# Five edits to a tuned decoder-layer kernel: one joint triangular substitution, w_o's rows behind the merge, a later T4, a moved subtraction, and a norm weight spread by products

## The chip, the cores and the metric

One core of a Trainium2 chip runs the whole kernel. The metric is device time in microseconds from start to end of one execution, as a median over runs.

The engines are named as in the profile's rows: PE is TensorE (matrix products), DVE is VectorE, ACT is ScalarE, POOL is GpSimd, and SP is the engine whose queue issues most of the transfers. Each engine works through its own instructions in their order, and waits at an instruction whose inputs or whose target buffer are not ready.

## The reference, cut to what matters

One decoder layer on 1024 tokens of width 1024, float32 in and out:

```python
u = rmsnorm(h, norm_mix_pre)
parts = split(u @ w_in)                  # q, k, v, z, b, a for mixer A; the rest for mixer B and the gates
ya = gdn_mixer(...)                      # causal conv over 4 tokens, silu, l2norm, gated delta rule
yb = nsa_mixer(...)                      # compressed, selected and sliding-window attention
mixed = (sigmoid(ga) * (ya @ w_a2d) + sigmoid(gb) * (yb @ w_b2d)) @ w_o
h = h + rmsnorm(mixed, norm_mix_post)
f = causal_dwconv(rmsnorm(h, norm_ffn_pre) @ w_up, conv_ffn) + conv_ffn_b
f = (gelu(f_gate) * f_val) @ w_down      # 2816 wide
h = h + rmsnorm(f, norm_ffn_post)
h = h + rmsnorm((p @ w_ple) * sigmoid(h @ w_ple_gate), norm_ple_post)
```

Inside the delta rule each chunk of a head needs the inverse of a unit lower triangular matrix, `lower + I`, with `lower = beta * (k k^T) * decay`.

## The kernel before, in words

A library schedules the instructions. The Python code is written in one order, and the library fixes the order on each engine by its own estimate of times; `tc.issue_after(x)` and `self.behind(x, ...)` keep what is written under them behind the instruction x. Pools of buffers (`bufs=n`) add waits where a buffer has to come free.

Every product is made three times (`mm3`, L394 to L396): each operand is split into a high part, rounded by ACT (`hi`, `whi`, `whl`), and a low part, the difference, made by DVE or POOL (`lo_of`, L362). The products high by high, low by high and high by low are added in PSUM. The low parts are where DVE and POOL come in for nearly every weight.

The stages that the change touches:

- **Start.** `mixers` loads x, and a copy of the first norm's weight for each of 128 partitions (`wbc`, 512 KB, by one transfer from ACT's queue). `norm_to_T` scales each token tile by it (`xs_u`, L414), and PE turns it (`pT_u`, L423).
- **Convolution and inverse.** For each of 12 feature tiles `conv` multiplies u by a 128-column slice of w_in (`pj`, 48 matmuls), evacuates the product with ACT (`y`, L570), adds three shifted taps on DVE (L573) and applies silu. Tiles 4 to 7 are k, 0 to 3 q, 8 to 11 v. `norms` sums the squares (`pss`). `gdn_small` makes the decay and gate numbers. `gdn_inverse32` makes, for each of 8 chunks of 128 tokens, the product k k^T (`pkk`), the decay factors (`E`, L948 on DVE, then exp on ACT, L953) and `L`, two DVE operations (L984, L985); it stores L in DRAM and reads its 32x32 diagonal blocks back, so that a block lies in 4 partitions and 32 blocks fill 128. Then it solves all blocks by forward substitution: 31 steps of one product (L1003) and one subtraction (L1005). It does this in two halves, chunks 0 to 3 in 64 partitions and chunks 4 to 7 in the other 64, with 62 DVE operations each, and its `yield`s let the convolution's work come between. The result goes to DRAM (`xd`) and is read back as blocks (`blk`). Four z gate tiles (`yz`, L611) are multiplied, then `gdn_prep(0)` combines the blocks with products (`pz`, `pt`, `pt1n`, L961 and L1041), and the scan over chunks begins.
- **Merge.** 16 tiles of 128 features by 512 tokens: a gate (ACT sigmoid, L795), gate times mixer A's product (DVE, L815), the product with w_b2d (`pab` on PE, 12 matmuls a tile), gate times it (L818), their sum (L819), and its high part `mxh` (ACT, L821) and low part `mxl` (POOL, for the last four tiles DVE). w_b2d comes in four slices (`stream`, L369, L373), the last two of them loaded inside this loop. `open_wo` loads the first NWO = 4 of w_o's 8 rows of tiles ahead of the loop, and `ffn` the other four behind it; `product` multiplies a token tile by rows 0 to 3 (half 0), for three token tiles, and then by rows 4 to 7.
- **Up-projection.** A Strassen-like scheme over pairs of feature tiles: seven products of half size, with weight sums `s1` to `s4` (`sums`) and token sums T2, T3, T4 (`turn`, L253 to L257). In `rest` pairs 0 to 2 are written out by hand, the others in a loop. `copy_of` (L106) copies a product out of PSUM on ACT before more is added to it; `c22` (L179) adds such a copy `r` to the product `n` on DVE before `p4` adds to n. `block_sum` (L234) makes sums of activations on POOL between products.
- **Down product.** `down` runs seven products of 11 steps each. A step loads an activation tile, splits it (`whl`, low part on DVE) and splits a weight tile (`wdhl`, low part on POOL, L362), and does 12 matmuls. Between the steps DVE makes weight differences in place: in product 4 (`dq`, written over `Q`) both `b12 -= ...` and `b21 -= t2` (L1567, L1568).

## Time and profile before

| What | Value |
|---|---|
| Median of 3 runs | 1929.55 us (1926.06 to 1931.4) |
| The profiled execution's own time | 1925.03 us |
| Its span, first to last instruction | 1923.3 us |
| Mean granted clock of TensorE | 0.986 of full speed |
| Busy: PE, DVE, ACT, POOL | 95%, 65%, 48%, 36% |
| Instructions | 25903 |

[...] A matmul of 128x512 shows as 0.39 us busy, but the next one starts 0.23 us later, since they overlap. A row of the timeline has the start, the busy time, the engine, the line, what is written and read, the shape, and in square brackets the idle time ahead and what ended it. The waits add these up: for a tile of PE, which operation on which engine it waited for. The table of stretches gives the busy time of each engine in a window.

### The profile page before, as it was taken

Reading aid. Unit: us, or ns where it says so; the run is one execution under the profiler, and the core shown is the slowest. Engines: PE = TensorE matmul, PEld = TensorE weight load, DVE = VectorE, ACT = ScalarE, POOL = GpSimd, SP = SyncE. Lnnn points to the kernel's source line nnn. Section 1 sums busy time; section 2 is a strip of 40 time slices with the busy share of each in tenths; the row PEclk is TensorE's granted clock in tenths of the full one; section 3 lists DMA queues with packets and bytes.
Section 4 is the critical chain, followed back from the end, with each engine's and each line's share of the span. In section 5 each row is a group of like instructions: output and inputs, shape, how many; then the busy total and the mean of one; then the engine's idle time right before and its main releaser. Section 6 shows DMA issues by size and latency. Waiting matters only on the chain. (4 is left out here: it accounts for less than half of the span.)

```text
span 1923.3 us, 25903 instructions
## 1 busy us (share of the span) xinstructions
PE 1834.8 (95%) x9307; PEld 1524.8 (79%) x9307; DVE 1242.5 (65%) x2353; ACT 919.2 (48%) x1817; POOL 700.2 (36%) x527
## 2 busy tenths in 40 slices
PE   7999989999999999999889998999999999899998
PEld 7888778988888888778768886787878877677786
DVE  5437934441367667766786589888777775948643
ACT  4344223323367667766664245444444444446432
POOL 2132112224122112331153146666666664645200
PEclk9999999999999999999999999999999999999999
DMA  5124333333310100110065212223332256246201
GB/s 168 34 86 116 91 92 89 93 88 92 102 45 18 45 29 34 57 44 13 22 216 169 98 55 94 98 94 101 107 99 93 99 206 243 77 138 219 76 34 44
DMA packets 182622, 178.67 MB, mean 93 GB/s; under 512 B 27549, under 2 KB 133342, under 8 KB 182494
## 3 DMA queue, kind: packets, MB, share of 16 engines
q1 hardware_dynamic: 180272, 170.33, 28.3%
q10 hardware_dynamic: 2222, 6.69, 0.9%
q8 instruction: 73, 1.20, 0.2%
q14 instruction: 55, 0.45, 0.1%
HBM read 132.65 MB, written 44.34 MB: 92 GB/s over the span
## 5 line engine op out<-in xcount | busy, mean ns | idle before, releaser
L394 PE MATMUL pj<-uh,whi 128*128 128x512 f32 x640 | 259.1, 405 | 7.4 <-DVE y L573 4.5
L395 PE MATMUL pj<-ul,whi 128*128 128x512 f32 x640 | 255.5, 399 | 0.0
L396 PE MATMUL pj<-uh,wlo 128*128 128x512 f32 x640 | 254.9, 398 | 0.0
L362 POOL TENSOR_TENSOR wlo<-raw,whi 128x1024 fp32r<-128x1024 f32 x48 | 117.5, 2449 | 312.1 <-ACT whi L373 268.3
L394 PEld LDWEIGHTS pj<-uh,whi 128*128 128x128 f32 x640 | 121.4, 190 | 35.4 <-issue 4.5
L362 POOL TENSOR_TENSOR whl<-s,whl 128x512 fp32r<-128x512 f32 x84 | 119.5, 1425 | 70.8 <-ACT whl L1393 69.0
L396 PEld LDWEIGHTS pj<-uh,wlo 128*128 128x128 f32 x640 | 121.2, 189 | 28.5
L395 PEld LDWEIGHTS pj<-ul,whi 128*128 128x128 f32 x640 | 121.4, 190 | 25.7
L362 POOL TENSOR_TENSOR whl<-raw,whl 128x512 fp32r<-128x512 f32 x71 | 114.6, 1621 | 62.6 <-ACT whl L1393 62.0
L362 POOL TENSOR_TENSOR wdhl<-wd,wdhl 128x512 fp32r<-128x512 f32 x66 | 100.0, 1524 | 82.2 <-ACT wdhl L1393 78.9
L362 DVE TENSOR_TENSOR whl<-araw,whl 128x512 fp32r<-128x512 f32 x77 | 89.8, 1173 | 54.9 <-ACT whl L1393 54.8
L394 PE MATMUL q<-mxh,whl 128*128 128x512 f32 (+1 forms) x272 | 105.9, 394 | 7.7 <-ACT r L106 7.7
L1275 ACT ACTIVATE Pt<-Pt,nm 128x640 f32<-128x640 f32 (+7 forms) x128 | 93.0, 729 | 36.4 <-DVE nm L1273 35.9
L1305 DVE TENSOR_TENSOR Tl<-pt,Th 128x512 fp32r<-128x512 f32 (+1 forms) x152 | 92.5, 616 | 21.7 <-ACT Th L1304 17.3
L396 PE MATMUL q<-mxh,whl 128*128 128x512 f32 (+1 forms) x272 | 105.1, 387 | 0.7 <-POOL whl L362 0.7
L395 PE MATMUL q<-mxl,whl 128*128 128x512 f32 (+1 forms) x272 | 105.3, 387 | 0.0
L1304 ACT ACTIVATE Th<-pt 128x512 fp32r<-128x512 f32 (+1 forms) x152 | 78.5, 539 | 42.7 <-PE po L1308 33.4
L373 ACT ACTIVATE whi<-raw 128x1024 fp32r<-128x1024 f32 x48 | 50.5, 1053 | 85.5 <-PE pj L395 55.5
L1301 PE MATMUL pt<-ident,Pt 128*128 128x128 f32 x528 | 83.4, 277 | 5.1 <-DVE Tl L1305 3.2
L1343 POOL TENSOR_TENSOR tm<-tm 128x128 f32<-128x128 f32 x32 | 14.8, 462 | 195.1 <-DVE tm L1341 155.3
L152 DVE SCALAR_TENSOR_TENSOR yg<-c,cv,yg 128x511 f32<-128x511 f32 (+2 forms) x88 | 76.9, 875 | 2.1 <-ACT yg L149 1.8
L152 DVE SCALAR_TENSOR_TENSOR yv<-c,cv,yv 128x1023 f32<-128x1023 f32 (+1 forms) x44 | 65.7, 1492 | 15.7 <-ACT yv L149 13.4
(548 smaller groups left out, 5181.4 us busy)
## 6 DMA issues: line engine op xcount, KB each, us to landing
raw<-in_w_up SPq DMA_DIRECT2D x44, 512.0 KB
raw<-in_w_in SPq DMA_DIRECT2D x40, 512.0 KB
araw<-acts SPq DMA_DIRECT2D x35, 512.0 KB
acts<-sd SPq DMA_DIRECT2D x44, 256.0 KB
gates_d<-yz SPq DMA_DIRECT2D x40, 256.0 KB
acts<-yv SPq DMA_DIRECT2D x33, 256.0 KB
gt<-gates_d SPq DMA_DIRECT2D x32, 256.0 KB
wd<-in_w_down SPq DMA_DIRECT2D x7, 1024.0 KB
```

The costliest lines, as they stand in the source:

```text
L152: self.body.nc.vector.scalar_tensor_tensor(y, src, w, y, ALU.mult, ALU.add)
L362: return eng.tensor_sub(lo, src, hi.bitcast(F32)).ins
L373: nc.scalar.activation(hi, raw, AF.Copy)
L394: nc.tensor.matmul(ps, lh, rh, start=start, stop=False, skip_group_check=more)
L395: nc.tensor.matmul(ps, lh, rl, start=False, stop=False, skip_group_check=more)
L396: nc.tensor.matmul(ps, ll, rh, start=False, stop=stop, skip_group_check=more)
L1275: nc.scalar.activation(Pt[:, hh, 0:nk], Pt[:, hh, 0:nk], AF.Exp, scale=2.0 ** -(h0 + hh + 1), bias=nm[:, br, hh:hh + 1], accum_out=rs[:, b ...
L1301: nc.tensor.transpose(pt[:, b, hh], Pt[:, hh, (b0 + b) * P:(b0 + b + 1) * P], self.ident)
L1304: nc.scalar.activation(Th[:, 0:m], pt[:, 0:m], AF.Copy)
L1305: nc.vector.tensor_sub(Tl[:, 0:m], pt[:, 0:m], Th[:, 0:m].bitcast(F32))
L1343: nc.gpsimd.tensor_add(tm[:, 0], tm[:, 0], tm[:, 1])
```

## The change

1. **Start.** The weight is loaded once, as 1x1024; two float32 products of a row of ones (1x128) with its halves spread it over the partitions in PSUM, and two DVE copies bring it to SBUF.
2. **Inverse.** `a_log` and `dt_bias` are loaded in the first stage. `gdn_small` becomes a generator that runs in three parts behind tiles 1 and 2. `E` of the noncausal kind is one ACT operation per head (Relu with the bias -gc). L is one DVE operation per head. All 8 chunks come first, two for each convolution tile, then one substitution over 128 partitions with three yields. `gdn_prep(0)` starts behind the second of the four z gate tiles.
3. **Merge.** NWO is 2; the last two slices of w_b2d are asked for earlier, and all these low parts are DVE's. Rows 2 to 7 of w_o load behind the merge, and `product` takes rows 0 to 3 one at a time over three token tiles.
4. **Up-projection.** Pair 1's s4 and the T4 turns are tied behind the copy r too, and pair 2 takes no block sum between its products.
5. **Down product.** `b21 -= t2` moves from product 4 to product 3.

The diff, cut to its core:

```diff
-NWO = 4
+NWO = 2
...
-        with body.behind(t3):
+        with body.behind(t3, self.copied):
             self.sums(b, (4,))
             t4 = self.turn(t2s, 4, range(4))
...
-                if self.todo:
+                if self.todo and n > 2:
...
-                    nc.scalar.dma_start(wbc, rows_to_all(io["norm_mix_pre"], DM))
+                    row, one = [self.wp.tile([P, DM], F32, name=n, tag=t, bufs=2)[0:1] for n, t in
+                                (("wrow", "raw"), ("one", "hi"))]
+                    nc.scalar.dma_start(row, rows_to_all(io["norm_mix_pre"], DM)[0:1])
+                    nc.vector.memset(one[:, 0:P], 1.0)
+                    for hf in range(2):
+                        c, ps = slice(hf * 512, hf * 512 + 512), self.psg.tile([P, 512], F32, name="pwb", tag="g")
+                        nc.tensor.matmul(ps, one[:, 0:P], row[:, c], start=True, stop=True)
+                        nc.vector.tensor_copy(wbc[:, c], ps)
                 self.norm_to_T(x, wbc, uh, ul, t, xw, self.psg, f"u{t}")
...
+            if inv:
+                with self.behind(last["DVE"], self.mm_last, *self.inv_last):
+                    next(inv, None)
             if n and order[n - 1] < 8:
                 norms(order[n - 1])
+            run_all(cv)
+            if n == 1:
+                self.gp = self.g1 = self.pool(ges, "gdn")
+                small = self.gdn_small(pss)
+            if n in (1, 2):
+                with self.behind(*last.values(), self.mm_last):
+                    next(small)
             if order[n - 1] == 7:
-                inv = self.gdn_inverse32()
-            if inv:
-                next(inv, None)
-            run_all(cv)
-        run_all(inv)
+                run_all(small)
+                inv, self.inv_last = self.gdn_inverse32(), ()
+        with tc.issue_after(last["DVE"]):
+            run_all(inv)
         jes.close()
         fes = ExitStack()
         psF = [self.pool(fes, "psF", 2, space=PSUM, side="right")]
...
             run_all(gate_tile(n))
+            if n == 1:
+                with tc.issue_after(self.mm_last):
+                    self.gdn_prep(0)
         NG = 8
-        self.gdn_prep(0)
...
+                if th and f % 2 and f0 + 4 < KD:
+                    wbs.append(self.stream(wbd, 0, 4, (f0 + 4) * P, 2 * P, nc.vector))
...
-            if f0 + 4 < KD:
-                wbs.append(self.stream(wbd, 0, 4, (f0 + 4) * P, 2 * P))
...
+            j = slice(c * H + h, c * H + h + 1)
+            if causal:
+                nc.vector.tensor_scalar(E[:, h], gr[:, h], self.gc[:, j], 0.0, ALU.subtract, ALU.min)
+            else:
+                nc.scalar.activation(E[:, h], gr[:, h], AF.Relu, bias=self.ngc[:, j])
...
+        for c in range(NC):
+            rk = self.row4(1, c, "qk", 2)
+            gr = self.row4(0, c, "gr", 2)
+            k = self.chunk(1, c)
+            nc.vector.tensor_mul(k, k, rk)
+            E = self.decay(c, gr, False)
+            pk = self.mm4(self.psgt("pkk"), k, k)
+            L = self.g1.tile([P, H, P], F32, name="L", tag="Z", bufs=2)
+            for h in range(H):
+                j = c * H + h
+                self.inv_last = (nc.vector.scalar_tensor_tensor(L[:, h], pk[:, h], self.beta[:, j:j + 1], E[:, h],
+                                                                ALU.mult, ALU.mult).ins,)
+            nc.sync.dma_start(self.ld[c], L)
+            for h in range(H):
+                p0 = (c * H + h) * 4
+                l = self.ld
+                nc.sync.dma_start(Ls[p0:p0 + 4], bass.AP(
+                    tensor=l.tensor, offset=l.offset + (c * P * H + h) * P,
+                    ap=[[32 * H * P + 32, 4], [H * P, 32], [1, 32]]))
+            if c % 2:
+                yield
+        nc.vector.memset(X, 0.0)
+        nc.vector.memset(X.rearrange("p i j -> p (i j)")[:, 0:1024:33], 1.0)
+        for j in range(31):
+            m, w = 31 - j, j + 1
+            t = tmp[:, 0:m * w].rearrange("p (a b) -> p a b", b=w)
+            nc.vector.tensor_mul(t, Ls[:, j + 1:, j].unsqueeze(2).to_broadcast([P, m, w]),
+                                 X[:, j, 0:w].unsqueeze(1).to_broadcast([P, m, w]))
+            nc.vector.tensor_sub(X[:, j + 1:, 0:w], X[:, j + 1:, 0:w], t)
+            if j in (8, 15, 22):
+                yield
+        nc.sync.dma_start(self.xd[0], X)
+        nc.vector.tensor_copy(Ls, X.rearrange("p i j -> p j i"))
+        nc.sync.dma_start(self.xd[1], Ls)
         nc.vector.memset(blk, 0.0)
         self.S, self.pre, self.pairs = None, {}, {}
...
+        self.wo = self.resident(self.pool(es, "woA"), "w_o", range(NWO), (self.nc.vector,))
...
-        for ks, tag in (((4, 5), "raw"), ((6,), "hi"), ((7,), "lo")):
+        for ks, tag in (((2, 3), "raw"), ((4, 5), "hi"), ((6, 7), "lo")):
...
-        for half in range(2):
+        for k in range(4):
             for t in range(3):
-                product(t, half)
+                product(t, (k,))
+        for t in range(3):
+            product(t, range(4, KD))
         under = {5: ((up.start, 0), (up.second, 0)), 6: ((up.plain, 0), (up.start, 1)), 7: ((up.second, 1),)}
         for t in range(NT):
...
         for j in product(4, t2, Q, False):
             with self.behind(up.lo):
                 nc.vector.tensor_sub(b12[:, j], b22[:, j], b12[:, j])
-                nc.vector.tensor_sub(b21[:, j], b21[:, j], t2[:, j])
         for t in range(4):
             nc.scalar.activation(facc[:, 4 + t, c0], Q[t], AF.Copy)
-        run(product(3, b11, Q, False))
+        for j in product(3, b11, Q, False):
+            with self.behind(up.lo):
+                nc.vector.tensor_sub(b21[:, j], b21[:, j], t2[:, j])
```

Where the change moves instructions, these are the places of which the prediction speaks.

TensorE at the start of the scan, before: `pj` are the last products of the fourth z gate tile, `pz` the first product of `gdn_prep(0)`, on the inverted blocks.

```order
991 L394 MATMUL pj<-uh,whi 128x512
992 L395 MATMUL pj<-ul,whi 128x512
993 L396 MATMUL pj<-uh,wlo 128x512
994 L961 MATMUL pz_2025<-blk 128x128 x4
995 L961 MATMUL pt_2032<-Z,blk 128x128 x4
996 L1041 MATMUL pt1n<-ident,TT 128x128 x4
997 L961 MATMUL pqk<-qT,kT 128x128 x4
998 L961 MATMUL pz_2068<-TT,blk 128x128 x4
```

The same place now:

```order
945 L396 MATMUL pj<-uh,wlo 128x512
946 L394 MATMUL pj<-uh,whi 128x512
947 L395 MATMUL pj<-ul,whi 128x512
948 L990 MATMUL pz_1862<-blk 128x128 x4
949 L396 MATMUL pj<-uh,wlo 128x512
950 L394 MATMUL pj<-uh,whi 128x512
951 L395 MATMUL pj<-ul,whi 128x512
```

`pz` stands 46 `pj` matmuls ahead of the end of the z gate tiles; 22 of them follow before `pt` and 23 more before `pt1n`.

ScalarE in the merge, before: `gt` are the gates' sigmoids, `mxh` the high parts of finished tiles, `whi` the high part of w_b2d's third slice, and `w_oh` those of w_o's rows.

```order
653 L821 ACTIVATE mxh_9719<-gt 128x512
654 L795 ACTIVATE gt<-gt 128x512 x2
655 L1372 ACTIVATE w_oh_9746<-raw 128x1024
656 L821 ACTIVATE mxh_9719<-gt 128x512
657 L795 ACTIVATE gt<-gt 128x512 x2
658 L821 ACTIVATE mxh_9715<-gt 128x512
659 L795 ACTIVATE gt<-gt 128x512 x3
660 L821 ACTIVATE mxh_9715<-gt 128x512
661 L373 ACTIVATE whi<-raw 128x1024
```

The same place now:

```order
664 L820 ACT_TABLE_LOAD
665 L820 ACTIVATE gt<-gt 128x512 x8
666 L848 ACTIVATE mxh_9676<-gt 128x512
667 L820 ACTIVATE gt<-gt 128x512
668 L848 ACTIVATE mxh_9676<-gt 128x512
669 L820 ACTIVATE gt<-gt 128x512
670 L848 ACTIVATE mxh_9680<-gt 128x512
671 L820 ACTIVATE gt<-gt 128x512
672 L373 ACTIVATE whi<-raw 128x1024
```

`whi` stands behind the third `mxh` instead of the sixth, and two `w_oh` are gone from between.

ScalarE in the up-projection, before: `T4h` are the high parts of T4's four turns, `r` the copy of pair 1's product p5 out of PSUM, and `p` and `u` are other such copies.

```order
742 L106 ACTIVATE u_11195<-q 128x512
743 L1393 ACTIVATE whl<-s_11243 128x512
744 L1393 ACTIVATE T4h<-t_11245 128x4x128
745 L106 ACTIVATE p_11224<-q 128x512
746 L1393 ACTIVATE whl<-raw 128x512
747 L1393 ACTIVATE T4h<-t_11250 128x4x128
748 L1393 ACTIVATE T4h<-t_11255 128x4x128
749 L106 ACTIVATE r<-q 128x512
```

The same place now:

```order
760 L106 ACTIVATE u_11156<-q 128x512
761 L1420 ACTIVATE whl<-s_11204 128x512
762 L106 ACTIVATE p_11185<-q 128x512
763 L1420 ACTIVATE whl<-raw 128x512
764 L106 ACTIVATE r<-q 128x512
765 L1420 ACTIVATE T4h<-t_11206 128x4x128
766 L1420 ACTIVATE T4h<-t_11211 128x4x128
767 L1420 ACTIVATE T4h<-t_11216 128x4x128
```

The copy `r` stands ahead of the first `T4h`, where three of the four stood ahead of it.

## Rows read from the trace of the kernel before

**Rows 1.** the page's first part, busy time and share of the span by engine

```profile
PE 1834.8 (95%) x9307; PEld 1524.8 (79%) x9307; DVE 1242.5 (65%) x2353; ACT 919.2 (48%) x1817; POOL 700.2 (36%) x527
```

**Rows 2.** waits of TensorE over the span: waited for, total us, times, longest us

```profile
PE pT_u L423 <- DVE ra_u L402: 9.4, 1, 9.4
PE q L394 <- ACT r L106: 7.7, 16, 2.8
PE dq L395 <- POOL wdhl L362: 6.1, 3, 5.7
PE pab L394 <- ACT whi L373: 5.7, 1, 5.7
PE pj L394 <- DVE y L573: 4.5, 3, 2.2
PE pz L961 <- DMA blk<-ld: 3.4, 1, 3.4
PE pj L394 <- ACT yz L611: 2.9, 2, 2.3
```

**Rows 3.** the table of stretches: busy us of each engine, granted clock, DMA

```profile
core 0: us, PE busy (x) PEld busy (x) DVE busy (x) ACT busy (x) POOL busy (x), PEclk, DMA share, GB/s
143.00:153.00 10.00, 9.89 (x35) 8.92 (x36) 7.17 (x15) 1.09 (x2) 0.00 (x0) 0.50 0.62 178
200.00:235.00 35.00, 30.41 (x129) 23.63 (x128) 32.12 (x67) 12.01 (x15) 6.26 (x4) 1.00 0.28 71
235.00:238.50 3.50, 3.50 (x9) 2.72 (x9) 3.36 (x5) 0.24 (x1) 1.70 (x1) 0.51 0.37 94
268.00:276.00 8.00, 6.53 (x32) 6.05 (x33) 1.15 (x2) 1.20 (x2) 0.00 (x0) 0.57 0.63 176
990.00:1000.00 10.00, 4.25 (x13) 3.03 (x12) 9.93 (x9) 7.55 (x13) 7.39 (x5) 0.66 0.62 208
1150.00:1177.00 27.00, 23.93 (x92) 18.86 (x90) 26.63 (x34) 15.49 (x23) 13.18 (x8) 0.87 0.20 59
1677.00:1689.00 12.00, 6.28 (x18) 4.59 (x17) 5.76 (x11) 2.82 (x5) 9.83 (x4) 0.72 0.22 70
1689.00:1721.00 32.00, 32.00 (x138) 25.75 (x137) 16.84 (x14) 14.52 (x26) 14.91 (x12) 1.00 0.27 77
```

**Rows 4.** VectorE by line, 60 to 300 us: busy us, mean ns, idle before

```profile
L1005 DVE TENSOR_TENSOR blk<-blk,tmp 64x31 f32<-64x31 f32 (+15 forms) x62 | 27.1, 438 | 1.8
L1003 DVE TENSOR_TENSOR tmp<-blk 64x31 f32<-64x31 f32 (+15 forms) x62 | 25.3, 408 | 3.0 <-DMA row<-rows_d 1.2
L948 DVE TENSOR_SCALAR E<-row,gc 128x128 f32<-128x128 f32 x44 | 10.0, 287 | 1.6 <-DMA row<-rows_d 1.6
L985 DVE TENSOR_TENSOR L<-L,beta 128x512 f32<-128x512 f32 x8 | 5.5, 681 | 0.1
```

**Rows 5.** timeline around the first scan product: start, busy us, what, idle before

```profile
252.16 1.12 DVE L1009 COPY blk<-blk 64x1024 f32<-64x1024 f32 x1
268.00 1.13 PE L961 MATMUL pz<-blk 128*128 128x128 f32 x8 [3.39 <-DMA blk<-ld]
```

**Rows 6.** timeline of the merge's end, TensorE, ScalarE, VectorE, GpSimd

```profile
1020.03 0.39 PE L396 MATMUL pab<-ybh,wlo 128*128 128x512 f32 x1
...
1027.17 1.06 ACT L1372 ACTIVATE w_oh<-raw 128x1024 fp32r<-128x1024 f32 x1 [1.24 <-DVE mxl L362]
1028.26 1.23 DVE L362 TENSOR_TENSOR w_ol<-raw,w_oh 128x1024 fp32r<-128x1024 f32 x1 [1.61 <-ACT w_oh L1372]
1029.31 5.77 POOL L362 TENSOR_TENSOR w_ol<-raw,w_oh 128x1024 fp32r<-128x1024 f32 x2 [9.19 <-ACT w_oh L1372]
```

**Rows 7.** timeline around the second pair's T4 product, VectorE and TensorE

```profile
1177.32 0.68 DVE L179 TENSOR_TENSOR c<-n,r 128x512 f32<-128x512 f32 x1
1178.05 0.50 PE L394 MATMUL n<-T4h,whl 128*128 128x512 f32 x1 [1.32 <-DVE c L179]
```

**Rows 8.** timeline of GpSimd in the down product

```profile
1674.64 11.48 POOL L362 TENSOR_TENSOR wdhl<-wdT,wdhl 128x512 fp32r<-128x512 f32 x3 [4.10 <-ACT wdhl L1393]
```

**Rows 9.** the page's groups: GpSimd's low parts of w_down, count, busy us, mean ns

```profile
L362 POOL TENSOR_TENSOR wdhl<-wd,wdhl 128x512 fp32r<-128x512 f32 x66 | 100.0, 1524 | 82.2 <-ACT wdhl L1393 78.9
```

More of the change, by code (lines that the diff above doesn't have):

```diff
@@ L572, in conv @@
                 d = 3 - j
[L573 to L574 removed]
+                last["DVE"] = nc.vector.scalar_tensor_tensor(y[:, d:], ps[:, 0:SEQ - d], cwt(j), y[:, d:], ALU.mult,
+                                                             ALU.add).ins
+            last["ACT"] = nc.scalar.activation(qkvT[i], y, AF.Silu).ins
+        last = {}
         order = [4, 5, 6, 7, 0, 1, 2, 3, 8, 9, 10, 11]
[L577 removed]
+        inv = small = None
         for n, i in enumerate(order):
@@ L1377, in open_wo, with token_mm @@
     def open_wo(self, es):
-        self.wo = self.resident(self.pool(es, "woA"), "w_o", range(NWO))
-    def token_mm(self, ps, t, w, half):
+        self.wo = self.resident(self.pool(es, "woA"), "w_o", range(NWO), (self.nc.vector,))
+    def token_mm(self, ps, t, w, ks):
         n = len(w)
         s = slice(t % 4 * P, t % 4 * P + P)
-        for k in (range(NWO), range(NWO, n))[half]:
+        for k in ks:
             mh, ml = [m[:, k % 4, s] for m in self.mx[k // 4, t // 4]]
@@ L1485, in ffn @@
             if t + 3 < NT:
-                for half in range(2):
-                    product(t + 3, half)
+                product(t + 3, range(KD))
             if t == 4:
```

69 lines of the change are left out of this document (15 added, 54 removed).

## The prediction, made before the changed kernel ran

> **What bounds the kernel now.** I read the page's first part, then the waits of TensorE, then the table of stretches, and only then the timelines of the places where the two agree. The first part says that TensorE (PE) is busy 95% of the span and every other engine 65% or less [rows 1]. So time can come from three things alone: PE's waits, stretches at half clock, and PE's own work, which the change leaves as it is but for two small products. The waits [rows 2] tell which engine ends PE's idleness: 9.4 us at the start, 10.2 us in the convolution and inverse stage (4.5 for `y`, 3.4 for the blocks read back, 2.3 in the longest wait for `yz`), one of 5.7 us in the merge, 2.8 us in the up-projection as the longest of 16 waits for `r`, and one of 5.7 us in the down product. [...]
>
> **The change, part by part.** The sum is made against the profiled execution's own 1925.0 us, which is 4.5 us under the median of the runs shown, 1929.55.
>
> *Start.* PE's first wait, 9.4 us, ends with the scaled tile. [...] Between +2.4 and -2.5 us I take **0**, the middle, since the two ends rest on rows equally near.
>
> *Convolution and inverse.* The substitution's two halves are 62 + 62 DVE operations, 27.1 + 25.3 us [rows 4]. They run on 64 partitions; joined, 62 run on 128. Is an operation on twice the partitions dearer? One of 512 elements on 128 partitions takes 681 ns, and 408 to 438 ns is the mean of operations of 31 to 256 elements on 64, so the time goes with elements per partition. The join saves half, 26.2 us of DVE. `E` moves 32 of 44 operations (10.0 us in all) to ACT: 7.3 us off DVE. L changes from two operations of 681 ns to four of 128x128, nearest to the 287 ns of E's shape [rows 4]: 1.36 against 1.15 a chunk, which I count as nothing.
>
> What does this free? DVE is busy 32.1 of 35 us from 200 to 235 [rows 3], and its chain ends with the copy at 252.16 + 1.12 = 253.3; `pz` runs at 268.0, 14.7 us later, the round trip through DRAM, after PE has waited 3.4 us [rows 5]. With 33.5 us less on DVE the chain ends near 219.8 and `pz` can run at 234.5. PE reached it at 264.6; it now comes 46 matmuls earlier in PE's order (46 x 0.232 = 10.7), and 13.4 us earlier if the waits for `y` and `yz` (6.8) and the half clock of 143 to 153 and 235 to 238.5 (half of 9.89 and of 3.50: 6.6) go: 240.5. So the blocks are 6 us ahead. What the stage loses now is 10.2 us of waits and 6.6 + 0.43 x 6.53 = 9.4 us of half clock, 19.6 us. I leave 3 us, one short wait and part of a half-clock stretch, since `pkk` and `pss` still stand together once: **-16.5 us**, between -19.6 and -6.
>
> *Merge.* PE waits for `whi` from 990 to 996 (busy 4.25 of 10 us, [rows 3]). ScalarE has it behind the sixth `mxh`, each of which waits for DVE's sums; now it is behind the third. The wait, 5.7 us, goes, and with it the half clock: 13 matmuls took 4.25 where 13 x 0.232 = 3.0 would do, 1.2 us, or 1.7 by the clock; 1.5. The low part, now DVE's, costs it 1.23 us [rows 6] and frees POOL of 2.9. But w_o's rows 2 to 7 now load behind the merge. Rows 0 and 1 cover 36 matmuls, 8.4 us, where rows 0 to 3 covered 16.8. Before, the last `pab` started at 1020.03, the first late high part at 1027.17, and its low part ended at 1028.26 + 1.23 = 1029.5, 9.2 us after PE went on [rows 6]. That is up to 1 us too late for row 2. Row 3 on POOL (5.77 for two, [rows 6]) is there at 1032.2, 12 us after, and needed at 13. So +1, between 0 (a shorter tail of `mxl`) and +6 (4 us of wait and the half clock after it): **-6.2 us**.
>
> *Up-projection.* The copy `r` goes ahead of the T4 turns on ACT, so PE's 2.8 us wait shrinks, and the half clock behind it: 92 matmuls from 1150 to 1177 would need 21.3 us and took 23.9, so 2.6. But DVE is busy 26.6 of those 27 us [rows 3], and the next thing PE needs is DVE's `c` at 1177.32, for which it waits 1.3 us even now [rows 7]. DVE has the same work up to there. PE then only waits there instead: **0**, between -5.4 (if `c` comes sooner too) and +3 (a longer wait with more half clock behind it). The block sums move by one pair on POOL, which does the same number of them by the time the next waits come; 0.
>
> *Down product.* DVE has two subtractions a step in product 4, and it ran them in one unbroken row while three `wdhl` on POOL took 11.48 us [rows 8], where one takes 1.52 on the mean [rows 9]. PE waited 5.7 us, and 18 matmuls that need 4.2 us took 6.28 [rows 3]. With 11 subtractions (0.68 us each, like L985) moved to product 3, DVE keeps pace with its steps and leaves gaps. Product 3's DVE was busy 16.84 of 32 us [rows 3]; 11 x 0.68 = 7.5 more fits. Of 7.8 us I count **-7.5**, between -7.8 and 0.
>
> [...]
>
> The sum: 0 - 16.5 - 6.2 + 0 - 7.5 = -30.2, so 1894.8 against the profiled execution, and 4.5 more against the median: **1899 us**.
>
> **The rivals.**
> - *The joint substitution still ends last.* It can't start before the eighth chunk's blocks are back; the first half could start at the fourth. For it: each chunk waits for a product, ACT and DVE in turn through the one buffer of E, and a round trip. Against it: the 6 us ahead. If it ends 10 us later than I have it, PE waits 4 us at `pz`, with 2.8 of half clock behind it, and half of the 6.8 us of `y` and `yz` waits stays: 10 us more, 1909.
> - *The T4 tie pays.* If DVE, with fewer stalls against POOL, has `c` 5 us sooner, the up-projection gives its 5.4 us: 1894.
> - *w_o's rows come late.* Rows 5 to 7 are loaded only when the last `pab` frees their buffers, and six high parts stand one behind the other on ACT at 1.06 us. If PE waits 4 us there, with the half clock of a 5.7 us wait, 1.5: 5.5 more, 1905.
> - *The down product's collision moves along.* If the subtractions hold POOL's `wdhl` up in product 3 as they did in product 4, the 7.5 us come back: 1907. Against it: they were two a step and are now one.
> - *Slower: the chunks' hand-over holds up the convolution.* ACT takes Relu for E in its own order; E has one buffer, so each chunk's Relu waits for DVE's last L of the chunk before, and behind it on ACT stand the evacuations of the next convolution tile, for which PE waits. The nearest price of such a hold is the wait and half clock at `pz`, 3.4 + 2.8 = 6.2 us; eight times that is 49.6 us, 19.4 more than the gain: 1949. It decides from 4.5 us a chunk on, where 8 x 4.5 eats the 30.2 and 5.8 beyond. Against it: ACT is idle for most of 143 to 153 [rows 3], and two chunks go with one convolution tile of 48 matmuls, 11 us.
>
> **How the numbers follow.** The forecast has 0.40, the late substitution 0.25, the T4 tie 0.12, w_o's rows 0.10, the moved collision 0.08, the slower case 0.05. A measurement of this kernel can tell about 0.3%, 5.8 us, from no change. Every case but the last ends 20 us or more below the median; two or three of them together, with the stage's gain at its low end of 6, come within 5.8 us of it. I give that 0.06, out of the first five; so faster 0.89, same 0.06, slower 0.05. The range reaches down to all gains in full (-42, 1887) less 4 for the scatter of the runs, 1883, and up to the late substitution with one more of the rivals, 1916; it leaves out the slower case and the same case with part of the rest, under 2 in 10.
>
> **What would show each step right or wrong.** Right: no wait of PE for `whi` and none for `wdhl` above 1 us; 62 substitution operations on 128 partitions with a mean near 0.42 us; `pz` without a wait over 1.5 us; the clock 1.00 in the merge and in the down product. The up-projection would show the wait for `r` shorter and the one for `c` of pair 1 longer, by about the same. Wrong: substitution operations near 0.8 us, a new wait of `pwo` for a `w_ol` of more than 2 us, a wait of `pz` of 4 us and more, or `y` and `yz` waits that stay at 6.8 us in all.

## The result and the profile after

| | Before | Changed |
|---|---|---|
| Median | 1929.65 us (1926.06 to 1931.4, 4 runs) | 1899.48 us (1899.06 to 1905.39, 4 runs) |
| The profiled execution's own time | 1925.03 us | 1899.06 us |

The ratio is 0.9853, with a 95% interval of 0.9829 to 0.9877: 1.5% faster, 30 us by the medians, and the number forecast, 1899. The two profiled executions differ by less, 25.97 us, where the terms of the sum made 30.2. The rest lies in the profiles' places among their runs: the median of before stood 4.6 us above its profile, that of the changed kernel only 0.4. So the match to within 1 us is luck: some terms are wrong, and their misses were hidden. Those terms are what the experiments are about.

The first view of the changed kernel is the page's first part, which answers to [rows 1]:

```profile
PE 1829.5 (96%) x9311; PEld 1518.5 (80%) x9311; DVE 1215.2 (64%) x2279; ACT 932.4 (49%) x1851; POOL 686.3 (36%) x524
```

VectorE has 27 us less work, ACT 13 more, and PE is still the engine that is busy nearly all the time. The waits of PE answer to [rows 2] (waited for, total us, times, longest us):

```profile
PE n L394 <- DVE c L179: 5.9, 2, 3.9
...
PE q L394 <- ACT r L106: 5.1, 16, 1.1
PE pwo L394 <- DVE gt L845: 3.5, 1, 3.5
...
PE pT_u L423 <- DVE xs_u L414: 3.0, 1, 3.0
...
PE pwb L534 <- DMA wrow<-in_norm_mix_pre: 2.8, 1, 2.8
PE pz L990 <- issue: 2.6, 1, 2.6
...
PE pj L394 <- DVE y L582: 1.4, 2, 0.8
...
PE dq L395 <- POOL wdhl L362: 0.2, 1, 0.2
```

Gone are the waits for `whi` (5.7) and for `wdhl` (5.7), and most of those for `y`. `pz` still waits 2.6 us ("issue" means that the profile shows nothing that it waited for; in the changed kernel's second profile the same wait, 2.4 us, is put down to the blocks read back). New are 3.5 us of `pwo`, the first product with w_o, for the multiplication that empties `pab` on VectorE, and, in the up-projection, 3.9 us for `c`, where `r` had the longest wait. The table of stretches (us, then busy us of each engine, granted clock as a share of full speed, DMA) shows what is left of the stretches at half clock, 0.50, of [rows 3]:

```profile
143.00:153.00 10.00, 10.00 (x44) 8.29 (x44) 6.08 (x9) 8.13 (x11) 1.07 (x1) 0.83 0.67 189
200.00:235.00 35.00, 34.24 (x147) 27.31 (x146) 31.61 (x56) 11.04 (x13) 7.43 (x3) 1.00 0.21 62
990.00:1005.00 15.00, 11.51 (x44) 8.70 (x44) 12.11 (x17) 5.76 (x10) 5.62 (x4) 0.90 0.51 175
1145.00:1166.00 21.00, 15.74 (x56) 11.78 (x55) 20.34 (x25) 9.81 (x15) 10.10 (x6) 0.84 0.21 63
1660.00:1672.00 12.00, 12.00 (x53) 9.65 (x52) 8.85 (x10) 5.51 (x10) 6.08 (x5) 1.00 0.43 123
1672.00:1704.00 32.00, 32.00 (x138) 25.76 (x137) 23.31 (x25) 16.88 (x29) 15.20 (x11) 1.00 0.51 168
```

The two stretches of the down product (the last rows) run without a gap at full clock; the merge's end and the up-projection do not.

To see where time went in all kernels alike, I measured each profile from the first product of one stage to the first of the next, in the timeline of PE. The marks are `pj` (first convolution product), `pu` (first in the scan), `pab` (first in the merge), `q` (first in the up-projection), `dq` (first in the down product), `dn` (first behind product 3) and the end of the last `pg`. All in us; the kernels below "changed" are those of the experiments.

| Kernel | start | convolution, inverse | scan, attention | merge, w_o | up-projection | down | rest | sum |
|---|---|---|---|---|---|---|---|---|
| before | 28.9 | 252.0 | 684.5 | 147.4 | 449.7 | 167.7 | 184.8 | 1915.1 |
| changed | 29.7 | 238.0 | 682.1 | 145.3 | 450.6 | 157.7 | 185.8 | 1889.2 |
| changed, again | 29.5 | 237.8 | 682.3 | 145.4 | 450.5 | 157.6 | 186.8 | 1889.8 |
| inverse undone | 29.1 | 254.9 | 684.3 | 144.0 | 450.4 | 157.8 | 186.1 | 1906.7 |
| two substitutions | 30.0 | 253.4 | 682.4 | 145.6 | 450.4 | 157.8 | 185.9 | 1905.5 |
| second E | 29.8 | 238.2 | 686.5 | 146.1 | 450.6 | 158.0 | 184.5 | 1893.7 |
| E on VectorE | 29.6 | 235.8 | 684.6 | 146.8 | 450.9 | 157.8 | 186.2 | 1891.8 |
| merge undone | 29.9 | 239.4 | 682.2 | 144.3 | 450.5 | 157.6 | 186.7 | 1890.6 |
| mxl on GpSimd | 29.6 | 238.4 | 682.0 | 141.7 | 450.4 | 157.7 | 186.5 | 1886.3 |
| both merge edits | 29.5 | 236.2 | 682.7 | 141.4 | 449.4 | 157.7 | 185.7 | 1882.7 |
| T4 undone | 30.2 | 238.3 | 682.9 | 145.2 | 449.9 | 158.2 | 184.7 | 1889.5 |
| second c | 29.6 | 238.0 | 683.6 | 146.5 | 453.9 | 157.7 | 185.8 | 1895.3 |
| down undone | 30.2 | 241.0 | 681.3 | 145.3 | 451.0 | 167.0 | 185.2 | 1900.9 |
| row by transfer | 29.0 | 238.3 | 689.6 | 146.7 | 450.4 | 156.9 | 185.8 | 1896.8 |

How much of a difference in a column is scatter? The two profiles of the changed kernel agree within 0.2 us in all but the last. But kernels with the same program in a stage spread further: 236.2 to 241.0 in the convolution column (the changed one and the six whose edits lie behind it), 681.3 to 686.5 in attention (without the row by transfer, whose order there differs in a piece of its own), 144.0 to 146.8 in the merge (the lowest is the kernel with the inverse undone), 449.4 to 451.0 in the up-projection, 156.9 to 158.2 in the down product, and 184.5 to 186.8 in the rest. Only what is larger is read as the edit's.

By columns the change brought +0.8, -14.0, -2.4, -2.1, +0.9, -10.0 and +1.0 us. Forecast were 0, -16.5, none for attention, -6.2, 0, -7.5 and none. The inverse and the down product are far outside the spread; attention, up-projection and rest are within it, and so is the size of the merge's -2.1, though the 147.4 of before lies above all kernels with the new merge code.

### The profile page after: what moved, and what is told of

Same layout as the page of the kernel before. It is cut to its first block, busy times and chain, and to the rows that moved or that the text cites. A ratio compares the mean times of both kernels' runs of the same rounds, so it can differ in the third digit from the quotient of the medians.

```text
span 1897.3 us, 25855 instructions
## 1 busy us (share of the span) xinstructions
PE 1829.5 (96%) x9311; PEld 1518.5 (80%) x9311; DVE 1215.2 (64%) x2279; ACT 932.4 (49%) x1851; POOL 686.3 (36%) x524
## 4 chain that ended last, share of the span: by engine, by line
PE 66%; DVE 9%; ACT 3%; issue 3%; POOL 2%; DMA 2%; SPq 0%; POOLq 0%; DVEq 0%; ACTq 0%
PE pj L394 5%; PE pj L395 4%; PE pj L396 4%; PE q L394 3%; PE q L396 3%; PE q L395 3%; PE pt L1328 2%; PE n L394 2%; PE n L395 2%; PE n L396 2%; PE dq L395 2%; PE dq L396 2%; PE ps L1294 2%; PE pg L396 2%; PE dq L394 2%
## 5 line engine op out<-in xcount | busy, mean ns | idle before, releaser
L395 PE MATMUL pj<-ul,whi 128*128 128x512 f32 x640 | 254.9, 398 | 0.0
L362 POOL TENSOR_TENSOR wlo<-raw,whi 128x1024 fp32r<-128x1024 f32 x46 | 110.5, 2403 | 324.6 <-ACT whi L373 264.5
```

The lines of the kernel that those rows point to most:

```text
L362: return eng.tensor_sub(lo, src, hi.bitcast(F32)).ins
L395: nc.tensor.matmul(ps, lh, rl, start=False, stop=False, skip_group_check=more)
```

## The experiments

All are edits of the changed kernel. Ratios are against the kernel before, which ran in each of the three series (medians 1931.58, 1934.57 and 1930.66 us), so times of different series are compared by ratio, or by the table above.

### Undo the inverse

The convolution and inverse stage of before, from `gdn_small` to `gdn_prep(0)`, in the changed kernel.

> The changed kernel with the convolution and inverse stage as it was before (two substitutions of 62 operations on 64 partitions, E on DVE, L in two operations, the first scan product behind all four z gate tiles); start, merge, up-projection and down product stay changed. Theory: the stage's gain stands alone, its 16.4 us come back and 1899.5 becomes 1914 to 1918, with the waits for y, for yz and of pz for the blocks in PE's list again (10 us together). Rival: part of the gain is given back later (a stage behind it waits for something that does not come sooner), then undoing costs less, 1905 to 1911.

Measured: 1916.04 us, ratio 0.9925 [0.99, 0.995]. The column is 254.9 against 238.0, +16.9, and no other column takes back more than 1.4 us. The theory holds: the stage's gain stands alone. (`y` waits 3.7 us, `yz` 2.9, `pz` 3.0 and 2.4.)

### Undo the merge

```diff
-NWO = 2
+NWO = 4
...
-                    wbs.append(self.stream(wbd, 0, 4, (f0 + 4) * P, 2 * P, nc.vector))
...
+            if f0 + 4 < KD:
+                wbs.append(self.stream(wbd, 0, 4, (f0 + 4) * P, 2 * P))
```

with the places of w_o's rows and the order of its products as before.

> The changed kernel with the merge as it was before (four of w_o's rows ahead of the loop, w_b2d's slices asked for late, their low parts on GpSimd, rows 0 to 3 of w_o multiplied token tile by token tile). Theory: the merge edit nets 2.6 us (7.7 saved, 5 lost at the first w_o products, which wait for PSUM banks that VectorE still has to empty), so this kernel is 2 to 4 us slower than the changed one, 1901.5 to 1903.5; the 5.7 us wait of pab for whi is back and the 3.5 us wait of pwo for VectorE is gone. Rival: the edit is worth the 6.2 us of the forecast and the wait of pwo comes from something else; then 1905 to 1907, with the wait of pwo still there.

Measured: 1898.96 us, ratio 0.9838 [0.9813, 0.9863]: not slower at all, and its merge column is 144.3, within the spread of the new code. Both theories miss. They took it that the undone code would bring the 5.7 us wait of before back. It did not. In ACT's timeline of this kernel the first `whi` stands behind the fourth `mxh`, at 974.11, where it stood behind the sixth before, and PE never waits for it. Its longest wait at `pab` is another, for the multiplication on VectorE that empties an earlier one:

```profile
970.01 0.63 ACT L846 ACTIVATE mxh<-gt 128x512 fp32r<-128x512 f32 x1 [1.15 <-DVE gt L844]
...
972.02 0.62 ACT L846 ACTIVATE mxh<-gt 128x512 fp32r<-128x512 f32 x1
...
974.11 1.04 ACT L373 ACTIVATE whi<-raw 128x1024 fp32r<-128x1024 f32 x1
977.57 0.63 ACT L846 ACTIVATE mxh<-gt 128x512 fp32r<-128x512 f32 x1 [2.42 <-DVE gt L844]
```

```profile
PE pab L394 <- DVE gt L843: 3.0, 1, 3.0
```

The merge's code is that of before, but the library made another order of it, from another past. So the column is 3.1 us shorter than before's with the old code too, and no gain of the merge edit as it stands can be seen: it shortens the loop (47.3 us from the first `pab` to the first `pwo`, against 50.6) and gives that back at the first products with w_o (98.0 us from there to `q`, against 93.7).

### Undo the T4 tie

```diff
-        with body.behind(t3, self.copied):
+        with body.behind(t3):
...
-                if self.todo and n > 2:
+                if self.todo:
```

> The changed kernel without the later T4 tie and with pair 2's block sum back. Theory: the wait only moved from the copy r on ACT to the sum c on VectorE, since VectorE is full there; 1898 to 1901, with a wait for r of 2 to 3 us and one for c of 1 to 2 where the changed kernel has 3.9 for c and 1.1 for r. Rival A: the tie pays, then 1903 to 1905. Rival B: the tie costs (its wait for c is longer than what it saved), then 1895 to 1897.

Measured: 1900.01 us, ratio 0.9844 [0.9813, 0.9876], the same as the changed kernel; the column is 449.9 against 450.6. The wait for `r` is back, 7.7 us with 2.8 as the longest, the same row as in [rows 2], and that for `c` shorter by one us:

```profile
PE n L394 <- DVE c L179: 5.4, 2, 2.9
```

The theory holds: the tie moves the wait and pays nothing.

### Undo the moved subtraction

```diff
         for j in product(4, t2, Q, False):
             with self.behind(up.lo):
                 nc.vector.tensor_sub(b12[:, j], b22[:, j], b12[:, j])
+                nc.vector.tensor_sub(b21[:, j], b21[:, j], t2[:, j])
...
-        for j in product(3, b11, Q, False):
-            with self.behind(up.lo):
-                nc.vector.tensor_sub(b21[:, j], b21[:, j], t2[:, j])
+        run(product(3, b11, Q, False))
```

> The changed kernel with both subtractions in product 4 of the down product again. Theory: VectorE's unbroken row holds up GpSimd's low parts again; PE waits 5 to 6 us for wdhl and part of what follows is at half clock: 8 to 9 us slower, 1907 to 1909. Rival: the collision is there in any order and the changed kernel pays it in product 3; then 1899 to 1901.

Measured: 1910.32 us, ratio 0.9893 [0.9868, 0.9918]; the column is 167.0 against 157.7, +9.3. The theory holds. GpSimd's timeline has the long row of [rows 8] again, and PE's waits show what it costs:

```profile
1660.42 11.47 POOL L362 TENSOR_TENSOR wdhl<-wdT,wdhl 128x512 fp32r<-128x512 f32 x3 [4.10 <-ACT wdhl L1420]
```

```profile
PE dq L395 <- POOL wdhl L362: 5.9, 2, 5.7
```

### Split the substitution

```diff
-        for j in range(31):
+        for i in range(62):
+            pp, j = slice(i // 31 * 64, i // 31 * 64 + 64), i % 31
...
-            if j in (8, 15, 22):
+            if i in (17, 30, 44):
```

with each operation on `pp`, 64 partitions.

> The changed kernel with its one substitution split into two of 62 operations on 64 partitions, both behind all eight chunks; all else as changed. Theory: the join carries the stage's gain. VectorE gets 62 more operations of about 0.43 us, 27 us, so its chain ends at 260 instead of 233 and the blocks are back at 275, where PE needs them between 246 and 257: 18 to 29 us slower, 1917 to 1928, in one wait of pz or of what follows. Rival: the gain comes from the parts around it (E on ACT, L in one operation, the scan's first product earlier), then 0 to 5 us slower, 1899 to 1904.

Measured: 1915.29 us, ratio 0.991 [0.9885, 0.9935]. The column is 253.4, +15.4. Less than the 18 to 29 expected, in part because the blocks came back 12 us after the last copy instead of 15, but the rival's 5 is far off: without the join the whole gain of the stage is gone, and the other edits in it bring 1.5 us (254.9 to 253.4), less than the column's spread. The copy that ends the chain and `pz`, in VectorE's and PE's timeline, and PE's stretch around them (granted clock 0.66):

```profile
256.58 1.12 DVE L1037 COPY blk<-blk 128x1024 f32<-128x1024 f32 x1
```

```profile
269.85 1.41 PE L990 MATMUL pz<-blk 128*128 128x128 f32 x5 [11.58 <-DMA blk<-ld]
```

```profile
255.00:285.00 30.00, 16.82 (x86) 15.00 (x85) 8.68 (x20) 6.98 (x11) 2.98 (x2) 0.66 0.43 121
```

### A second buffer for E

```diff
-        E = self.g1.tile([P, H, P], F32, name="E", tag="E", bufs=1)
+        E = self.g1.tile([P, H, P], F32, name="E", tag="E" if causal or c % 2 == 0 else "o", bufs=1)
```

> The changed kernel with a second buffer for the noncausal E (even chunks in E's own, odd chunks in the buffer of o, which is free there). Theory: the 15.1 us in which VectorE stands idle ahead of L (8.5 for E, 6.6 for pkk) come from the hand-over of the one buffer, and are why the substitution ended at 233.1 and not at the forecast 219.8. With two, at least 8 us of that idle time go, the substitution ends by 225, pz's wait of 2.6 us and the half clock behind it go: 1895 to 1897.5. Rival: the chunks wait for the rows' transfers or for ACT's turn among the convolution's work, and E's buffer decides nothing: the idle time stays within 3 us, 1898 to 1901.

Measured: 1905.72 us, ratio 0.9859 [0.9837, 0.988]. VectorE's idle time ahead of L falls from 15.1 to 10.0 us, between the two expectations. But the substitution's first operation moves only from 190.99 to 190.09, and its copy ends at 234.1, no sooner than 233.1:

```profile
190.09 0.21 DVE L1030 TENSOR_TENSOR tmp<-blk 128x31 f32<-128x31 f32 x1 [2.15 <-DMA blk<-ld]
```

So the one buffer made VectorE wait, and the substitution still starts when the last chunk's blocks are back from DRAM. What the buffer alone is worth is not shown, since the order on PE changed with it: the last chunks' `pkk` come 3.7 us later than in the changed kernel (PE's timelines, the changed kernel first):

```profile
174.84 2.03 PE L990 MATMUL pkk<-kT 128*128 128x128 f32 x16
```

```profile
178.50 1.95 PE L990 MATMUL pkk<-kT 128*128 128x128 f32 x16
```

The wait of `pz` falls to 0.5 us, and the convolution column stays all the same (238.2). The attention column is the longest but one, 686.5, with the changed kernel's order from 305 us on. Three stretches of it show why: from 725 to 745 us, for one, the second-E kernel (first row) has part of the time at half clock and 111 matmuls done, where the changed kernel's second profile (second row) has full clock and 119:

```profile
725.00:745.00 20.00, 17.73 (x111) 15.38 (x109) 14.30 (x60) 15.80 (x45) 7.44 (x6) 0.91 0.12 40
```

```profile
725.00:745.00 20.00, 17.59 (x119) 15.22 (x117) 15.98 (x66) 17.29 (x52) 9.55 (x9) 1.00 0.12 40
```

The other two are from 775 to 790 us (0.89, against 1.00 in the changed kernel's second profile) and from 805 to 825 us (0.91).

### E on VectorE again

```diff
-                nc.scalar.activation(E[:, h], gr[:, h], AF.Relu, bias=self.ngc[:, j])
+                nc.vector.tensor_scalar(E[:, h], gr[:, h], self.gc[:, j], 0.0, ALU.subtract, ALU.max)
```

> The changed kernel with the noncausal E on VectorE again, all else as changed. Theory: the last chunk's blocks land at 191, and that sets the start of the substitution, not VectorE's work before it; VectorE stands idle 15.1 us ahead of L, so E's 7.3 us fit there, the substitution ends within 2 us of 233 and the time stays: within 3 us of the changed kernel, 0.9840 to 0.9870. Rival (the step of the prediction): VectorE's chain is one row of work, so its end moves by 7.3 us, and pz waits 10 us instead of 2.6, with half clock behind: 9 to 11 us slower than the changed kernel, 0.990 to 0.991.

Measured: 1901.96 us, ratio 0.985 [0.9837, 0.9864], beside 0.9848 for the changed kernel in the same series. VectorE has the 32 operations of E back, 7.4 us, and its idle time ahead of L halves. These are VectorE's lines from 60 to 300 us (busy us, mean ns, idle before) and the copy:

```profile
L1014 DVE SCALAR_TENSOR_TENSOR L<-pkk,beta,E 128x128 f32<-128x128 f32 x32 | 9.0, 344 | 7.3 <-PE pkk L990 5.0 <-ACT E L982 2.3
L978 DVE TENSOR_SCALAR E<-row,gc 128x128 f32<-128x128 f32 x32 | 7.4, 295 | 1.6 <-DMA row<-rows_d 1.5
```

```profile
231.27 1.11 DVE L1036 COPY blk<-blk 128x1024 f32<-128x1024 f32 x1
```

The copy is 0.7 us sooner with the work back on VectorE. The theory holds and the prediction's step falls: those microseconds were not on the chain that sets the end.

### The low parts of the last merge tiles on GpSimd

```diff
-                self.lo_of(ml, gb, mh, nc.vector if f0 == KD - 2 else nc.gpsimd)
+                self.lo_of(ml, gb, mh, nc.gpsimd)
```

> The changed kernel with the low parts mxl of the merge's last four tiles on GpSimd instead of VectorE. Theory: the first w_o products wait 3.5 us for PSUM banks because VectorE's last multiplications out of pab stand behind two mxl, each of which waits for ACT; without them the banks are free some 3 us sooner: the wait falls under 1 us and the half clock of 3.4 us behind it goes, 1894 to 1896.5. Rival: the gates' transfers and the w_o rows set the pace there, or GpSimd's slower mxl hold up the products of rows 6 and 7; the wait moves on and the time stays, 1898 to 1901.

Measured: 1897.31 us, ratio 0.9818 [0.9796, 0.984]; the merge column is 141.7, -3.6. The wait of `pwo` falls from 3.5 to 1.3 us and the half clock behind it is gone (the stretch has 1.00 where it had 0.90). The theory holds, with a remainder:

```profile
990.00:1005.00 15.00, 13.67 (x58) 10.54 (x57) 11.86 (x14) 6.53 (x11) 11.58 (x8) 1.00 0.64 206
```

```profile
PE pwo L394 <- DVE gt L845: 1.3, 1, 1.3
```

These four low parts were VectorE's in the kernel before too. Whether GpSimd would have helped the old merge code as much was not tried.

### Both merge edits

The edit above, and the first two rows of w_o together for each token tile:

```diff
-        for k in range(4):
+        for ks in ((0, 1), (2,), (3,)):
             for t in range(3):
-                product(t, (k,))
+                product(t, ks)
```

> The changed kernel with the low parts mxl of the last four merge tiles on GpSimd, and with the first two rows of w_o multiplied together for each token tile before the next token tile begins, so that the first two PSUM banks carry 12 products instead of 6. Theory: with mxl on GpSimd alone 1.3 us of wait for VectorE stayed at the first products; it goes, and the kernel is 4 to 6 us faster than the changed one, the best of all, 0.9815 to 0.9835. Rival: that last wait is for something else or moves to the next bank; then the same as mxl on GpSimd alone, 2.5 to 3.5 us faster than the changed kernel.

Measured: 1895.44 us, ratio 0.9816 [0.9803, 0.983], 6.3 us less than the changed kernel in the same series (1901.7). The merge column is 141.4, so 0.3 less than with GpSimd's low parts alone, where 1.3 were expected. By the times of the same products in the two profiles, 1.5 us are gained at the first products with w_o, and 1.4 were lost ahead of them, at half clock from 956 to 958 us (granted clock 0.59 from 955.5 to 958.9, against 1.00 at the same products). The edits explain 4.0 of the 7.1 us between the two profiles; the rest lies in columns with the same program, within their spread. The stretch of the first w_o products has PE busy throughout, at full clock:

```profile
990.00:1005.00 15.00, 15.00 (x66) 12.21 (x66) 11.28 (x14) 6.97 (x12) 11.12 (x8) 1.00 0.70 226
```

This is the fastest kernel run by its median, and its interval lies below that of the changed kernel in the same series, 0.9833 to 0.9864; by time it can't be told from GpSimd's low parts alone (0.9818).

### A second buffer for c

```diff
-        p.c2 = self.up.tile([P, SEQ], F32, name="c2", tag="c2", bufs=1)
+        p.c2 = self.up.tile([P, SEQ], F32, name="c2", tag="c2", bufs=2)
...
             self.gate_lo(b)
+            self.c22(b)
             self.gated(a)
             self.keep(a)
         self.p3(b)
-        self.c22(b)
         self.p4(b)
```

> The changed kernel with two buffers for the sum c of the up-projection, and pair 1's sum c = n + r written ahead of pair 0's gate work; in VectorE's order that sum then stands some 15 operations earlier. Theory: PE's waits for c (5.9 us, 3.9 the longest) come from c's single buffer, which holds the sum behind the reading of the pair before; they fall under 2 us and half of 6.8 us at half clock goes with them: 1892 to 1896. Rival: VectorE is full from 1118 to 1166 (47 of 48 us), so whatever goes later in its order is waited for instead (a low part, a sum of weights, a PSUM bank): 1898 to 1901.

Measured: 1904.12 us, ratio 0.9856 [0.983, 0.9882]; the column is 453.9, +3.3. The wait for `c` fell to 1.5 us, and this took its place:

```profile
PE q L396 <- POOL whl L362: 6.3, 2, 5.6
```

The rival holds: where VectorE is full, what is moved ahead makes something else late, here a low part on GpSimd.

### The norm's weight by one transfer

```diff
-                    nc.scalar.dma_start(row, rows_to_all(io["norm_mix_pre"], DM)[0:1])
...
-                        nc.vector.tensor_copy(wbc[:, c], ps)
+                    nc.scalar.dma_start(wbc, rows_to_all(io["norm_mix_pre"], DM))
```

> The changed kernel with the first norm's weight spread by one transfer of 512 KB again, without the products with ones. Theory: the two ways cost the same within 1 us: psm's first product at 12.3 instead of 13.0 and the first convolution product at 28.9 instead of 29.7, 0 to 1 us faster, within 0.1% of the changed kernel. Rival: the transfer delays the other x tiles; then the end of psm is 1 to 3 us later.

Measured: 1908.09 us, ratio 0.9881 [0.9865, 0.9897], 6.4 us slower than the changed kernel in the same series. At its own place the theory is right: the first `pj` comes at 29.0 instead of 29.5. For the whole time it is wrong. The loss is 7.3 us in attention (689.6 against 682.3), and 3.1 beyond the spread of that column. By the times of the same products in both profiles, 4.3 of it come between 539 and 618 us, where the order differs. PE waits there for the maximum `mx` of a row of scores five times, 2.8 us in all, where the changed kernel waits once, 0.5:

```profile
PE ps L1286 <- DVE mx L1289: 2.8, 5, 1.0
```

The order that the library made there differs. One piece of the difference on PE, this kernel's rows with -, the changed kernel's with + (`ps` are scores, `pf` turns finished rows back):

```
-L1348 MATMUL pf<-vsc,Tc 128x64 x2
-L1357 MATMUL pf<-ident,oT 128x128
+L1294 MATMUL ps<-kst,qs 128x256
+L1295 MATMUL ps<-kst,qs 128x256
```

That 4.3 us are lost there, and that the order there is another, is shown; which of the moved instructions costs them was not tried. The rest of the 7.3, most of it at 735 and 815 us, is where the second-E kernel lost its 4.4 with the order unchanged, so I count it as scatter.

### The changed kernel again

> The changed kernel itself, again, beside the three below on one chip. Every theory: 0.983 to 0.988 of the kernel before. Its profile shows which waits come back (of pz, of pwo for VectorE, in the down product) and which wander from execution to execution: the up-projection of three other kernels, whose program is the same there, showed its longest wait at m for a low part of GpSimd (2.9 us) where the first profile had it at n for c (3.9 us).

Measured: 1901.7 us, ratio 0.9848 [0.9833, 0.9864]. The waits of `pz` (2.4) and `pwo` (3.8) are there again. In the up-projection the same program has another longest wait:

```profile
PE m L396 <- POOL whl L362: 2.9, 1, 2.9
...
PE n L394 <- DVE c L179: 2.3, 2, 1.2
```

In the first profile these were 0.5 and 5.9. The column is 450.5 and 450.6 us: the wait wanders among VectorE's and GpSimd's results, and its sum stays.

## Why the prediction was right, and where it was not

**Start: forecast 0.** At its own place +0.8 us, between its ends of +2.4 and -2.5. No run shows either end by itself. What the runs show in their place: the two products with the row of ones are four matmuls of about 1.06 us each, from 2.8 to 6.5 us, the two copies take 0.68 us each, and the first `pj` comes at 29.7 and 29.5 in the changed kernel's two profiles and at 29.0 with the transfer. What the prediction did not hold is what the edit is worth in this kernel: 6.4 us, of which 4.3 come with another order in the attention stage. The sum had no term for attention at all. The prediction read the order at the three places that it spoke of, and took every other stage as fixed. From before to after this did no harm: the column moved by -2.4, within its spread.

**Convolution and inverse: forecast -16.5, measured -14.0.** The join carries it, as said: without it 15.4 us come back. But the step that gave the end of the chain fell. It took the 33.5 us of saved work off VectorE's chain, 253.3 to 219.8, as if VectorE would stay busy. It ended at 233.1. These are VectorE's lines from 60 to 300 us, and its timeline and PE's where the substitution starts, ends and is used:

```profile
L1032 DVE TENSOR_TENSOR blk<-blk,tmp 128x31 f32<-128x31 f32 (+15 forms) x31 | 14.9, 481 | 0.9
L1030 DVE TENSOR_TENSOR tmp<-blk 128x31 f32<-128x31 f32 (+15 forms) x31 | 14.2, 459 | 3.2 <-DMA blk<-ld 2.4
L1014 DVE SCALAR_TENSOR_TENSOR L<-pkk,beta,E 128x128 f32<-128x128 f32 x32 | 9.0, 343 | 15.1 <-ACT E L982 8.5 <-PE pkk L990 6.6
```

```profile
183.59 1.12 DVE L1014 SCALAR_TENSOR_TENSOR L<-pkk,beta,E 128x128 f32<-128x128 f32 x4
...
190.99 1.80 DVE L1030 TENSOR_TENSOR tmp<-blk 128x31 f32<-128x31 f32 x1 [2.37 <-DMA blk<-ld]
...
231.97 1.12 DVE L1036 COPY blk<-blk 128x1024 f32<-128x1024 f32 x1
```

```profile
248.49 0.35 PE L990 MATMUL pz<-blk 128*128 128x128 f32 x1 [2.55 <-issue]
```

The price of an operation on twice the partitions was nearly right: 481 and 459 ns against 438 and 408 [rows 4], so 29.1 us for 62, against 26.2 forecast. What was wrong is the start. The last L is written at 183.59, its blocks are back at 190.99, and from there the substitution and the convolution's taps between take until 231.97. Before, the first half, begun at 167.22, filled that time; now VectorE idles through it, 15.1 us ahead of L alone. Two experiments show this: 7.4 us more work on VectorE ahead of L did not make the copy's end later (232.4 against 233.1), while the split substitution, whose 62 more operations stand behind the last L, made it 24.6 us later (257.7). What sets the last L itself, one step further back, was not tried; its product `pkk` stands behind a convolution tile in PE's order, and with a second buffer for E it came later. The 3 us that the term leaves, with `pkk` and `pss` standing together as a reason, are the author's estimate, and no run shows them by themselves: in the changed kernel the two stand together from 139.1 to 144.5, and the granted clock is 1.00 from 137 to 143 and 0.83 from 143 to 153; with the split substitution it is 1.00 from 130 to 170. The first rival, the substitution that ends last, was so right in its mechanism and too dear in its size: the chain ended 13.3 us later than forecast, and the 6 us in hand became 2.6 us of wait. Half of 9.89 and of 3.50 is 6.7, not the 6.6 of the prediction, which changes nothing. Over the whole column the profiles account for the gain: PE idles 6.8 us in it instead of 14.1, and the mean granted clock is 0.99 instead of 0.96. The slower rival did not happen: PE never waited for a convolution product because of E.

**Merge: forecast -6.2, measured -2.1.** This step failed. The wait for `whi` went, as forecast, but "Rows 0 and 1 cover 36 matmuls, 8.4 us" asked only whether w_o's rows were there. They were. The PSUM banks were not: the new order goes to the second token tile after 6 products, 1.4 us, where it was 24 before, and its banks were still full of `pab`. VectorE emptied them at its own pace, behind low parts that waited for ACT. PE's and VectorE's timelines at that place:

```profile
998.23 0.40 PE L396 MATMUL pwo<-w_oh,mxl 128*128 128x512 f32 x1
1002.12 0.79 PE L394 MATMUL pwo<-w_oh,mxh 128*128 128x512 f32 x1 [3.50 <-DVE gt L845]
```

```profile
998.05 0.69 DVE L362 TENSOR_TENSOR mxl<-gt,mxh 128x512 fp32r<-128x512 f32 x1 [1.70 <-ACT mxh L848]
998.66 0.69 DVE L845 TENSOR_TENSOR gt<-pab,gt 128x512 f32<-128x512 f32 x1
...
1000.77 0.69 DVE L362 TENSOR_TENSOR mxl<-gt,mxh 128x512 fp32r<-128x512 f32 x1 [0.70 <-ACT mxh L848]
1001.38 0.68 DVE L845 TENSOR_TENSOR gt<-pab,gt 128x512 f32<-128x512 f32 x1
```

The matmul at 1002.12 starts 0.06 us after the multiplication at 1001.38 ends, and takes 0.79 instead of 0.40, at half clock (granted 0.50 from 1002.1 to 1005.5). With the low parts on GpSimd the 3.6 us come back. And with the old merge code the column was no longer, 144.3: so the -2.1 can't be put down to this edit. In both kernels the wait for `whi` is gone; the old code lost it by another order of the library.

**Up-projection: forecast 0, measured +0.9**, within the spread. Right, and by the reason given: VectorE is full (20.34 of 21 us from 1145 to 1166), so the wait goes from `r` to its next result. That this result was to be `c` is right for one execution of two. The rival that the T4 tie pays is refuted by its undoing.

**Down product: forecast -7.5, measured -10.0.** The mechanism is right, and undoing it costs 9.3. By the times of the same products in both profiles, 8.4 us are gained in the stretch from 1677 to 1689 that the term was read from, 0.9 more than forecast, and 1.5 ahead of it, most of that at 1666, where PE of the kernel before waited 0.75 us for a low part of VectorE. The rival, that the collision moves along, happened in part, and cost TensorE nothing (busy 32.00 of 32 us from 1672 to 1704, at 1.00). VectorE's moved subtractions and GpSimd's low parts, from their timelines in product 3:

```profile
1680.08 1.77 DVE L1601 TENSOR_TENSOR wd<-wd,wdT 128x512 f32<-128x512 f32 x1
...
1689.30 0.68 DVE L1601 TENSOR_TENSOR wd<-wd,wdT 128x512 f32<-128x512 f32 x1
```

```profile
1681.82 1.77 POOL L362 TENSOR_TENSOR wdhl<-wd,wdhl 128x512 fp32r<-128x512 f32 x1 [0.53 <-ACT wdhl L1420]
1684.64 1.29 POOL L362 TENSOR_TENSOR wdhl<-wd,wdhl 128x512 fp32r<-128x512 f32 x1 [1.04 <-ACT wdhl L1420]
```

Where they meet, a subtraction takes 1.77 us instead of 0.68, and a low part 1.77 instead of 1.29. VectorE loses 1.09 us there and GpSimd 0.48; why they hold each other up is not shown. With one subtraction a step, three of the 11 take 1.77 to 1.79 us and no low part of the product more than 1.77; with two in an unbroken row, in the kernel with the edit undone, three low parts took 11.47 us.

**The sum.** The misses are +0.8, +2.5, -2.4, +4.1, +0.9, -2.5 and +1.0: 4.4 us in all (4.2 before rounding), and the medians' own offset of 4.2 hid them. Only the inverse's, the merge's and the down product's are larger than 1 us and on an edit's place. The inverse's 2.5 is less than that column spreads by, and the 2.6 us wait of `pz` is not shown to be its cause: with a second buffer for E that wait is 0.5 us and the column the same.

## What to carry to other kernels

Work taken off an engine shortens a chain only where the engine is busy all along it: find the last arrival that the chain must wait for, and count from there. When a product is put into a new order, ask for each step not only whether its operands are there but whether its output bank is empty, and who empties it. And where a library orders the instructions, an edit also acts in stages that it does not touch, so compare stage by stage, from first product to first product, know how far a stage spreads between kernels that share it, and do not take the undone code for the old order.

## What was not expected

The attention stage took from 681.3 us (the down product undone, mean granted clock 1.00) to 686.5 us (second E, 0.99) with the same order from 305 us on, by whether stretches of it ran at half clock. The same program put its longest up-projection wait at `n` for `c` (3.9 us) in one execution and at `m` for a low part (2.9 us) in another, with the stage's length within 0.1 us. And single steps of the substitution seem to be held up by GpSimd as the subtractions are: its first product took 1.80 us while a low part of GpSimd ran from 190.34 to 192.74, where the next product, of nearly twice the elements, took 0.22.
